# Low parts of weights and rotary products: from GpSimd to VectorE in a two-layer diffusion trunk

## The chip, the cores and the metric

The kernel runs on one core of a Trainium2 chip. The metric is the device time of one execution in microseconds; the number to predict is the median of several runs. Engines are named as in the profile: PE (TensorE), ACT (ScalarE), DVE (VectorE), POOL (GpSimd) and SP (SyncE, which issues the DMAs here).

## The reference

Two layers run over 256 latent tokens (`x`) and 256 context tokens (`h`), 1024 wide, in float32. Each layer is three sub-layers: a feed-forward layer, a mixing layer, a feed-forward layer.

```python
x = ffn_sublayer(x, mod_x, 0, *f0)
h = ffn_sublayer(h, mod_h, 0, *f0)

ax = adaln_in(x, norm_pre[l, 1], mod_x[:, 3], mod_x[:, 4])
ah = adaln_in(h, norm_pre[l, 1], mod_h[3], mod_h[4])
uv_x, qb_x, qc_x, kb_x, vb_x, kc_x, vc_x = jnp.split(ax @ w_in[l], SPLITS, axis=-1)
...
qb_x = apply_rope(qb_x.reshape(b_, l_, B_HEADS, 2, B_QK_DIM), cos_b, sin_b)
...
o_a = chunk_gmlp(uv_x, ...)            # gated spatial mixing
o_b = diff_post(diff_attention_latent(qb_x, k_all, v_all, lam), ...)
o_c = swa_latent(qc_x, kc_x, vc_x, kc_h, vc_h, sink)
mix_x = jnp.concatenate([o_a, o_b, o_c], axis=-1) @ w_out[l]
x = adaln_out(x, mix_x, norm_post[l, 1], mod_x[:, 5], 1.0)
...
x = ffn_sublayer(x, mod_x, 2, *f1)     # (silu(y @ wg) * (y @ wu)) @ wd, half residual weight
```

The rotary embedding is `x * cos + rot * sin`, on latent queries and keys alone. In the second layer the context gives keys and values only.

## The kernel before

**Three products for one.** Every weight tile of 2048 columns is loaded by SP into a staging buffer (`stg`, three of them) and then split: ACT writes the rounded high part `hi` (line 240), and a subtraction writes the low part `lo = full - hi` (`split_lo`, line 101). A matrix product is then three matmuls into one PSUM bank: `hi` by `Yh`, `lo` by `Yh`, `hi` by `Yl`, where `Yh` and `Yl` are the activations split in the same way. `acc3` issues the three terms at lines 250 and 254, `acc3_multi` at 263 (the second term), 269 and 271. `split` cuts a tile with eight or more blocks into four pieces and smaller ones into two; for each piece it issues the ACT copy and then the subtraction.

**Who subtracts.** The subtraction is on DVE, but where `share=True` is passed the first piece of the tile is on POOL: for the tiles of the input projection (`cols`, and the three tiles `wv` of the values), for those of the output projection of the first layer (`chunk` in `mixing`), and for the first two pairs of gate and up tiles of every feed-forward layer but the first (`two` in `ffn`, lines 614 and 618). A piece is 512 columns in most of them, 1024 for the output projection, 640 for `wv`, 256 for the narrow key tile.

**Rotary.** `rope_evac` (line 701) takes a 256 column product out of PSUM with ACT, shuffles it on DVE (704), multiplies the shuffled copy by the sine on DVE (705), multiplies the original by the cosine on POOL (706), and adds the two on DVE (707).

**What else POOL does.** The power -1/2 of each norm on one to four columns (lines 424, 839, 920, 1187), the product of one half of a feed-forward output with its gate row (line 521, `hf` 0), and the DMAs that store the gate rows (379).

**Softmax and residual on DVE.** A unit of differential attention reduces the scores on DVE (800), lets ACT take the exponent (802), combines two sums in two instructions on one or two columns (805, 806) and blends the two exponent tiles (808); PE then transposes the blend (781), ACT takes it out of PSUM (783), and PE multiplies it by the values (818). The windowed attention does the same with lines 872 to 880 and 895. `residual` adds the scaled product to the stream (439) and scales the normed stream (447), with a root from POOL ahead of each; `turn_y` transposes the result on PE (461) and splits it again (466, 471, 101).

**Order.** Each engine runs its own queue in order. The order within a queue is fixed when the program is built, from program order, from the `high_priority` blocks (which hold the splits of the input projection, `first=True`), and from the estimates of the planner that lays out the queues. On PE the attention units, rotary and transposes are interleaved with the projections by a clock written out in the kernel (`later`, `tick`, `task`).

Of the kernel before, what the change touches and what calls it, by code (L numbers as in the profile page):

```python
# [15 lines left out]
ALU = mybir.AluOpType  # L16
# [9 lines left out]
KB = D // P  # L26
# [37 lines left out]
def trunk(ctx: ExitStack, tc: tile.TileContext, x, c, cx, c_ctx, w_mod, b_mod, norm_pre, norm_post,  # L64
          w_gate, w_up, w_down, w_in, w_out, v_gain, w_s, b_s, diff_lambda, diff_subln, swa_sink,
          rope, out):
    nc = tc.nc
# [29 lines left out]
    def f32(ap):  # L97
        return ap.bitcast(F32)

    def split_lo(lo, full, hi, eng=nc.vector):  # L100
        eng.tensor_tensor(lo, full, f32(hi), op=ALU.subtract)  # L101


    evq, clk, busy = [], [0.0], [False]
# [114 lines left out]
                return split(v, *args[1:], **kw)  # L219
        return split(stage(*args), *args[1:], **kw)  # L220

    def split(v, nk, ncol, pair=False, into=None, share=False, pool=False):
        if into is not None:
            hi, lo = into
        else:
            hi = wsp.tile([P, 2048], F32R, tag="hi", name=nm("hi"))[:, 0:nk * ncol].rearrange(
                "p (k c) -> p k c", k=nk)
            lo = wsp.tile([P, 2048], F32R, tag="lo", name=nm("lo"))[:, 0:nk * ncol].rearrange(
                "p (k c) -> p k c", k=nk)
        if pair:  # L230
            v4 = v.rearrange("p k (v g d) -> p k v g d", v=2, g=2)
            for g in range(2):
                hv = hi[:, :, g * P:(g + 1) * P].rearrange("p k (v d) -> p k v d", v=2)
                lv = lo[:, :, g * P:(g + 1) * P].rearrange("p k (v d) -> p k v d", v=2)
                nc.scalar.activation(hv, v4[:, :, :, g, :], AF.Copy)
                split_lo(lv, v4[:, :, :, g, :], hv)
            return hi, lo
        cut = [0, nk // 4, nk // 2, nk // 2 + nk // 4, nk] if nk >= 8 else [0, nk // 2, nk]
        for a, b in zip(cut, cut[1:]):
            nc.scalar.activation(hi[:, a:b, :], v[:, a:b, :], AF.Copy)  # L240
            split_lo(lo[:, a:b, :], v[:, a:b, :], hi[:, a:b, :],
                     nc.gpsimd if pool or (share and a == 0) else nc.vector)
        return hi, lo

    def acc3(o, terms):
# [299 lines left out]
                task(("y", s), turn_y(ys, nxt, st, s[0], *((pb, T_LATE, 1.2) if s == order[-1] else (pa,))))  # L545


    def gate_up(l, e, cs, into=None, share=False):
        return (wchunk([(0, 256, w_gate[l, e, :, cs:cs + 256])], KB, 256, into=into, share=share),
                wchunk([(0, 256, w_up[l, e, :, cs:cs + 256])], KB, 256, share=share))  # L550

    def gate_up_one(l, e, cs):
        return wchunk([(0, P, w_gate[l, e, :, cs:cs + P]), (P, 256, w_up[l, e, :, cs:cs + P])], KB, 256)
# [1 line left out]
    def ffn(l, e, streams, nxt, first=None, out_order=None):  # L555
        j = 2 * e
        full = (streams[-1][0], streams[0][1])
        n = full[1] - full[0]
# [33 lines left out]
        for pi, (f0, nf) in enumerate(PHASES):  # L592
            Uh = big.tile([P, KB, NT], F32R, tag="Uh", name=nm("Uh"))
            Ul = big.tile([P, KB, NT], F32R, tag="Ul", name=nm("Ul"))
            for fp in range(0, nf, 2):
                cs = (f0 + fp) * P
                two = pi == 0 and fp == 0 and not first
                if pi == 0 and fp == 2 and not first:
                    continue
                rows = nxt is None  # L600
                if first and pi == 0 and fp == 0:
                    for i in range(3):
                        hidden(first[i], first[3 + i], i, full)
                    step()
                    continue
                if first and pi == 0 and fp == 2:
                    gu = [pa(), pa()]
                    w = gate_up_one(l, e, cs + P)
                    for i in range(2):
                        acc3(gu[i], yterms(w, i * P, full))  # L610
                    hidden(gu[0], gu[1], 3, full)
                    step()
                    continue
                wg, wu = gate_up(l, e, cs, share=two)
                if two:
                    into = [t[:, 4:8, :].rearrange("p a (b c) -> p (a b) c", b=2)
                            for t in (Uh, Ul)]
                    second = gate_up(l, e, cs + 256, into, True)
                    for s in range(2) if rows else streams:
                        drain(("y", s))  # L620
                        for f, (g_, u_) in ((0, (wg, wu)), (2, second)):
                            if rows:
                                gu = pa()
                                acc3_multi([(gu[:, c0:c0 + 256], rterms(w, s), c0 == 0)
                                            for w, c0 in ((g_, 0), (u_, 256))])
                                task("u", hidden_rows(gu, f, s))
                                continue
                            gus = [pa(), pa()]
                            groups = []
                            for w, c0 in ((g_, 0), (u_, 256)):  # L630
                                for i in range(2):
                                    groups.append((gus[i][:, c0:c0 + 256], yterms(w, i * P, s),
                                                   c0 == 0))
                            acc3_multi(groups)
                            for i in range(2):
                                hidden(gus[i][:, 0:256], gus[i][:, 256:512], f + i, s)
                else:
                    for i in range(2):
                        g = pa()
                        acc3(g[:, 0:n], yterms(wg, i * P, ys))  # L640
                        u = pa()
                        acc3(u[:, 0:n], yterms(wu, i * P, ys))
                        hidden(g[:, 0:n], u[:, 0:n], fp + i, full)
                step()

            drain("u")
            down(l, e, pi, f0, nf, Z, Uh, Ul, out_order or streams, nxt)
# [40 lines left out]
    def mixing(l, streams, qstreams, nxt):  # L688
# [4 lines left out]
        full = (0, NT)  # L693
# [4 lines left out]
        W = w_in[l]  # L698


        def rope_evac(dst, ps, scale):
            nc.scalar.activation(dst, ps, AF.Copy, scale=scale)
            sh = wk.tile([P, 256], F32, tag="t256", name=nm("shf"))
            nc.vector.stream_shuffle(sh, dst, shmask)
            nc.vector.tensor_tensor(sh, sh, ropet[:, 1, :], op=ALU.mult)
            nc.gpsimd.tensor_tensor(dst, dst, ropet[:, 0, :], op=ALU.mult)
            nc.vector.tensor_tensor(dst, dst, sh, op=ALU.add)

        def fm(w, f0, s):
# [10 lines left out]
                nc.scalar.activation(dst[:, SEQ:NT], ps[:, o:o + CTX], AF.Copy, scale=scale)  # L720

        def cols(c0, n, into=None):
            return wchunk([(0, n, W[:, c0:c0 + n])], KB, n, into=into, share=True, first=True)

        tmpw = big.tile([P, 2, KB, 256], F32R, tag="Ul", name=nm("tmpw"))
        wkq = []
# [21 lines left out]
        def rows_of(k0, n, c0, w):  # L748
            return W[k0 * P:(k0 + n) * P, c0:c0 + w]

        wv = [wchunk([(0, 512, rows_of(k0, n, VB0, 512)), (512, 640, rows_of(k0, n, VC0, P))], n, 640,
                     share=True, first=True)
              for k0, n in ((0, 3), (3, 3), (6, 2))]

        def tok_terms(ws, tb, c0, c1):
# [370 lines left out]
            return (QK[:, 4 + 2 * i:6 + 2 * i, SEQ:NT] if i < 2 else CU[:, 2 * i - 3:2 * i - 1, SEQ:NT])  # L1126

        def chunk(hf, i):
            return wchunk([(0, 512, w_out[l, i * 512:(i + 1) * 512, hf * 512:(hf + 1) * 512])], 4, 512,
                          share=True)  # L1130

        def oterms(ws, tb):
            return [(Yh[:, k, ycols(tb)], Yl[:, k, ycols(tb)], ws[k // 4][0][:, k % 4, :],
# [195 lines left out]
```

## Time and profile before

| | |
|---|---|
| median of 3 runs | 1762.75 us (1761.02 to 1763.5) |
| the profiled execution: its own time, its span | 1762.98 us, 1761.2 us |
| PE matmul busy | 1722.4 us, 98% |
| DVE, ACT, POOL busy | 1190.4, 696.3, 168.9 us |
| mixing layer of layer 0, attention and output (480 to 600 us) | PE busy 113.37 of 120 us |
| end of mixing of layer 1 and first tiles of its feed-forward layer (1550 to 1575 us) | PE busy 21.63 of 25 us |

How to read it: the span is that of the instructions; the time of a run has 1.78 us around it. PE works almost throughout, so what a change can give back is the time in which PE waits. Those waits lie at the edges of stages and in the mixing layers. A row of a timeline has the start, the time taken, the engine, the line, out<-in, the shape and the count of instructions merged; in brackets stands the idle time of the engine before it and what ended that.

### The profile page before, as it was taken

Reading aid. Unit: us, or ns where it says so; the run is one execution under the profiler, and the core shown is the slowest. Engines: PE = TensorE matmul, PEld = TensorE weight load, DVE = VectorE, ACT = ScalarE, POOL = GpSimd, SP = SyncE. Lnnn points to the kernel's source line nnn. Section 1 sums busy time; section 2 is a strip of 40 time slices with the busy share of each in tenths; the row PEclk is TensorE's granted clock in tenths of the full one; section 3 lists DMA queues with packets and bytes.
Section 4 is the critical chain, followed back from the end, with each engine's and each line's share of the span. In section 5 each row is a group of like instructions: output and inputs, shape, how many; then the busy total and the mean of one; then the engine's idle time right before and its main releaser. Section 6 shows DMA issues by size and latency. Waiting matters only on the chain.

```text
span 1761.2 us, 24837 instructions
## 1 busy us (share of the span) xinstructions
PE 1722.4 (98%) x9663; PEld 1449.9 (82%) x9663; DVE 1190.4 (68%) x2174; ACT 696.3 (40%) x1480; POOL 168.9 (10%) x185
## 2 busy tenths in 40 slices
PE   7999999999999999999999999999999999999998
PEld 5788888879977789888888898888888897689997
DVE  4876876775667576768766576777864756765555
ACT  4332322244376562333232442332223526655443
POOL 0000000021322120000000210000001321010000
PEclk9999999999999999999999999999999999999999
DMA  9654554543131143445545233655544133226552
GB/s 336 207 173 160 188 197 144 167 150 109 60 103 52 57 137 125 162 163 189 191 144 185 75 120 123 205 178 191 180 144 167 48 108 120 73 90 197 192 191 84
DMA packets 197105, 259.20 MB, mean 147 GB/s; under 512 B 8234, under 2 KB 132348, under 8 KB 196988
## 3 DMA queue, kind: packets, MB, share of 16 engines
q1 hardware_dynamic: 195452, 257.56, 44.3%
q8 instruction: 76, 1.25, 0.3%
q14 instruction: 41, 0.34, 0.1%
q0 software_dynamic: 1536, 0.05, 0.0%
HBM read 256.49 MB, written 1.10 MB: 146 GB/s over the span
## 4 chain that ended last, share of the span: by engine, by line
PE 63%; DVE 7%; ACT 2%; issue 2%; POOL 1%; DMA 1%; POOLq 0%; DVEq 0%; ACTq 0%
PE pa L250 19%; PE pa L254 9%; PE pb L269 4%; PE pb L271 4%; PE pb L263 4%; PE pa L263 4%; PE pa L271 4%; PE pa L269 4%; PE pb L250 3%; DVE lo L101 2%; PE pb L254 1%; PE pa L797 1%; PE pc L818 1%; PE pc L895 1%; DVE S L439 1%
## 5 line engine op out<-in xcount | busy, mean ns | idle before, releaser
L101 DVE TENSOR_TENSOR lo<-stg,hi 128x512 fp32r<-128x512 f32 (+3 forms) x476 | 367.0, 807 | 192.5 <-ACT hi L240 122.8
L240 ACT ACTIVATE hi<-stg 128x512 fp32r<-128x512 f32 (+3 forms) x496 | 318.4, 702 | 329.6 <-PE pa L263 97.2
L250 PE MATMUL pa<-Yh,hi 128*128 128x512 f32 (+1 forms) x1168 | 415.0, 365 | 0.0
L250 PE MATMUL pa<-Yl,hi 128*128 128x512 f32 (+1 forms) x1168 | 413.8, 364 | 0.0
L357 DVE SCALAR_TENSOR_TENSOR acc<-stg,sT,acc 128x512 f32<-128x512 f32 x448 | 305.2, 743 | 4.0 <-DMA stg<-in_w_mod_dram 4.0
L254 PE MATMUL pa<-Yh,lo 128*128 128x512 f32 (+1 forms) x1168 | 257.8, 363 | 0.0
L250 PEld LDWEIGHTS pa<-Yh,hi 128*128 128x128 f32 x1168 | 220.5, 189 | 36.6 <-issue 2.9
L250 PEld LDWEIGHTS pa<-Yl,hi 128*128 128x128 f32 x1168 | 220.5, 189 | 35.0 <-issue 1.2
L254 PEld LDWEIGHTS pa<-Yh,lo 128*128 128x128 f32 x1168 | 202.4, 189 | 34.3
L570 ACT ACTIVATE Uh<-ha 128x512 fp32r<-128x512 f32 (+1 forms) x92 | 50.7, 551 | 296.4 <-DVE ha L568 296.4
L263 PE MATMUL pb<-hi,Ul 128*128 128x512 f32 x400 | 156.9, 392 | 0.0
L271 PE MATMUL pb<-lo,Uh 128*128 128x512 f32 x400 | 155.9, 390 | 0.8 <-DVE lo L101 0.8
L269 PE MATMUL pb<-hi,Uh 128*128 128x512 f32 x400 | 155.8, 391 | 0.1
L568 DVE TENSOR_TENSOR ha<-ha,pa 128x512 f32<-128x512 f32 (+1 forms) x91 | 53.0, 583 | 79.5 <-PE pa L254 79.0
L269 PE MATMUL pa<-Yh,hi 128*128 128x256 f32 x368 | 92.0, 285 | 0.0
L271 PE MATMUL pa<-Yl,hi 128*128 128x256 f32 x368 | 91.3, 283 | 0.0
L271 PEld LDWEIGHTS pb<-lo,Uh 128*128 128x128 f32 x400 | 75.1, 188 | 16.6 <-DVE lo L101 1.3
L263 PEld LDWEIGHTS pb<-hi,Ul 128*128 128x128 f32 x400 | 75.1, 188 | 16.5 <-issue 1.2
L269 PEld LDWEIGHTS pb<-hi,Uh 128*128 128x128 f32 x400 | 75.2, 188 | 16.0 <-DVE Z L503 0.5
L566 ACT ACTIVATE ht<-pa 128x512 f32<-128x512 f32 (+1 forms) x91 | 46.3, 510 | 104.1 <-PE pa L254 81.8
L379 POOL DMA_DIRECT2D gate<-gr x48 | 24.3, 513 | 603.7 <-DVE gr L376 535.3
L567 DVE SCALAR_TENSOR_TENSOR ha<-ht,pa 128x512 f32<-128x512 f32 (+1 forms) x91 | 52.9, 581 | 37.2 <-ACT ht L566 36.4
(299 smaller groups left out, 2732.4 us busy)
## 6 DMA issues: line engine op xcount, KB each, us to landing
stg<-in_w_mod_dram SPq DMA_DIRECT2D x64, 1024.0 KB, 5.0
stg<-in_ffn_w_gate_dram SPq DMA_DIRECT2D x42, 1024.0 KB, 5.2
stg<-in_ffn_w_up_dram SPq DMA_DIRECT2D x42, 1024.0 KB, 5.1
stg<-in_ffn_w_down_dram SPq DMA_DIRECT2D x32, 1024.0 KB, 5.0
stg<-in_w_in_dram SPq DMA_DIRECT2D x14, 1024.0 KB, 4.8
stg<-in_ffn_w_down_dram SPq DMA_DIRECT2D x16, 768.0 KB, 4.4
mst<-in_w_mod_dram SPq DMA_DIRECT2D x16, 512.0 KB, 7.6
stg<-in_w_out_dram SPq DMA_DIRECT2D x8, 1024.0 KB, 6.4
```

The source lines that it names most:

```text
L101: eng.tensor_tensor(lo, full, f32(hi), op=ALU.subtract)
L240: nc.scalar.activation(hi[:, a:b, :], v[:, a:b, :], AF.Copy)
L250: nc.tensor.matmul(o, lhsT=ah, rhs=r, start=(i == 0), stop=(i == n - 1))
L254: nc.tensor.matmul(o, lhsT=al, rhs=bh, start=(i == 0), stop=(i == n - 1))
L263: nc.tensor.matmul(o, lhsT=al, rhs=bh, start=False, stop=last, skip_group_check=True)
L269: nc.tensor.matmul(o, lhsT=ah, rhs=bh, start=(first and k == 0), stop=False, skip_group_check=True)
L271: nc.tensor.matmul(o, lhsT=ah, rhs=bl, start=False, stop=False, skip_group_check=True)
L357: nc.vector.scalar_tensor_tensor(a, v[:, k, :], sc, a, op0=ALU.mult, op1=ALU.add)
L566: nc.scalar.activation(t, g, AF.Tanh, scale=0.5)
L567: nc.vector.scalar_tensor_tensor(a, t, 1.0, g, op0=ALU.add, op1=ALU.mult)
L568: nc.vector.tensor_tensor(a, a, u, op=ALU.mult)
L570: nc.scalar.activation(uh, a, AF.Copy)
```

## The change

`split_lo` loses its engine argument and always runs on DVE; `split` loses `share` and `pool`; `wchunk` callers lose `share=True`; and the cosine product of the rotary embedding goes to DVE. Nothing is removed from the computation, and shapes, tiles, DMAs and PE's instructions are as before. 37 subtractions and 22 rotary products move. POOL keeps the roots, the gate products of line 521, and its DMAs.

```diff
-    def split_lo(lo, full, hi, eng=nc.vector):
-        eng.tensor_tensor(lo, full, f32(hi), op=ALU.subtract)
+    def split_lo(lo, full, hi):
+        nc.vector.tensor_tensor(lo, full, f32(hi), op=ALU.subtract)
...
-    def split(v, nk, ncol, pair=False, into=None, share=False, pool=False):
+    def split(v, nk, ncol, pair=False, into=None):
...
-            split_lo(lo[:, a:b, :], v[:, a:b, :], hi[:, a:b, :],
-                     nc.gpsimd if pool or (share and a == 0) else nc.vector)
+            split_lo(lo[:, a:b, :], v[:, a:b, :], hi[:, a:b, :])
...
-                wg, wu = gate_up(l, e, cs, share=two)
+                wg, wu = gate_up(l, e, cs)
...
-                    second = gate_up(l, e, cs + 256, into, True)
+                    second = gate_up(l, e, cs + 256, into)
...
-            nc.gpsimd.tensor_tensor(dst, dst, ropet[:, 0, :], op=ALU.mult)
+            nc.vector.tensor_tensor(dst, dst, ropet[:, 0, :], op=ALU.mult)
...
-            return wchunk([(0, n, W[:, c0:c0 + n])], KB, n, into=into, share=True, first=True)
+            return wchunk([(0, n, W[:, c0:c0 + n])], KB, n, into=into, first=True)
...
-                     share=True, first=True)
+                     first=True)
...
-            return wchunk([(0, 512, w_out[l, i * 512:(i + 1) * 512, hf * 512:(hf + 1) * 512])], 4, 512,
-                          share=True)
+            return wchunk([(0, 512, w_out[l, i * 512:(i + 1) * 512, hf * 512:(hf + 1) * 512])], 4, 512)
```

## Rows read from the trace of the kernel before

**Rows 1.** The first part of the page: busy time of each engine, share of the span, instructions.

```profile
PE 1722.4 (98%) x9663; PEld 1449.9 (82%) x9663; DVE 1190.4 (68%) x2174; ACT 696.3 (40%) x1480; POOL 168.9 (10%) x185
```

**Rows 2.** POOL's instructions grouped by line and shape over the whole span: busy time and mean ns of one, then the idle time before them. All but the second row are instructions that move.

```profile
L101 POOL TENSOR_TENSOR lo<-stg,hi 128x512 fp32r<-128x512 f32 x19 | 28.3, 1489 | 35.4 <-ACT hi L240 35.4
L424 POOL TENSOR_TENSOR r<-v,negh 128x1 f32<-128x1 f32 x38 | 26.4, 694 | 114.8 <-DVE v L422 108.5 <-DMA stg<-in_w_in_dram 6.3
...
L101 POOL TENSOR_TENSOR lo<-stg,hi 128x640 fp32r<-128x640 f32 x6 | 13.6, 2271 | 28.1 <-ACT hi L240 28.1
L706 POOL TENSOR_TENSOR QK<-QK,ropet 128x256 f32<-128x256 f32 x16 | 13.3, 850 | 13.4 <-DVE shf L704 13.4
L101 POOL TENSOR_TENSOR lo<-stg,hi 128x1024 fp32r<-128x1024 f32 x5 | 12.2, 2446 | 32.9 <-ACT hi L240 32.9
...
L706 POOL TENSOR_TENSOR CU<-CU,ropet 128x256 f32<-128x256 f32 x6 | 5.7, 946 | 27.1 <-DVE shf L704 27.1
L101 POOL TENSOR_TENSOR Ul<-stg,Uh 128x512 fp32r<-128x512 f32 x3 | 4.3, 1426 | 2.0 <-DVE zg L1083 1.2 <-ACT Uh L240 0.8
L101 POOL TENSOR_TENSOR tmpw<-stg,tmpw 128x512 fp32r<-128x512 f32 x2 | 2.9, 1446 | 0.5 <-ACT tmpw L240 0.5
...
L101 POOL TENSOR_TENSOR lo<-stg,hi 128x256 fp32r<-128x256 f32 x2 | 1.5, 731 | 58.8 <-ACT hi L240 58.8
```

**Rows 3.** DVE's instructions in the same view: the subtractions by shape, the two rotary instructions that stand on either side of POOL's product, and a product of two 128x256 tiles elsewhere (line 921).

```profile
L101 DVE TENSOR_TENSOR lo<-stg,hi 128x512 fp32r<-128x512 f32 x369 | 242.7, 699 | 115.5 <-ACT hi L240 63.3 <-PE pa L254 51.4 <-PE pb L254 0.8
L101 DVE TENSOR_TENSOR lo<-stg,hi 128x1024 fp32r<-128x1024 f32 x87 | 106.7, 1240 | 31.4 <-PE pa L254 16.9 <-ACT hi L240 14.3 <-ACT hi L235 0.2
...
L705 DVE TENSOR_TENSOR shf<-shf,ropet 128x256 f32<-128x256 f32 x22 | 18.6, 871 | 0.1
...
L707 DVE TENSOR_TENSOR QK<-QK,shf 128x256 f32<-128x256 f32 x16 | 10.0, 652 | 0.1
...
L921 DVE TENSOR_TENSOR VG<-VG,r 128x256 f32<-128x256 f32 x6 | 2.5, 425 | 4.8 <-POOL r L920 4.8
...
L101 DVE TENSOR_TENSOR lo<-stg,hi 128x640 fp32r<-128x640 f32 x2 | 1.7, 826 | 1.9 <-ACT hi L240 1.6 <-issue 0.3
```

**Rows 4.** Three of PE's waits over the whole span: who waited for whom, us in total, times, longest.

```profile
PE pa L781 <- DVE p L808: 2.9, 4, 1.5
...
PE pa L271 <- DVE lo L101: 2.0, 2, 1.5
...
PE pb L461 <- DVE Z L447: 1.7, 2, 1.4
```

**Rows 5.** Busy time by stretch: PE, PEld, DVE, ACT, POOL, each with its count, then the granted clock of PE (1.00 is 2.4 GHz, 0.50 is 1.2 GHz), DMA share, GB/s. Attention and output of the mixing layer of layer 0; attention of layer 1; the end of mixing of layer 1 with the first feed-forward tiles behind it; and two pieces of 10 us of the last.

```profile
480.00:600.00 120.00, 113.37 (x753) 89.56 (x752) 84.86 (x232) 81.75 (x251) 22.17 (x17) 1.00 0.18 62
1456.00:1512.00 56.00, 51.64 (x337) 41.37 (x337) 41.52 (x92) 37.33 (x95) 10.93 (x9) 1.00 0.34 114
...
1550.00:1575.00 25.00, 21.63 (x148) 20.25 (x147) 18.02 (x26) 13.24 (x33) 7.22 (x6) 0.93 0.48 158
...
1560.00:1570.00 10.00, 7.13 (x53) 6.52 (x54) 8.36 (x15) 3.91 (x9) 2.64 (x3) 1.00 0.91 310
1570.00:1580.00 10.00, 10.00 (x73) 10.00 (x73) 4.33 (x10) 3.67 (x10) 0.00 (x0) 0.83 0.27 79
```

**Rows 6.** Timeline at 522 us, windowed attention in layer 0: a POOL subtraction, a DVE instruction on one column beside it, and PE's wait three steps on.

```profile
522.54 2.39 POOL L101 TENSOR_TENSOR lo<-stg,hi 128x1024 fp32r<-128x1024 f32 x1 [4.04 <-ACT hi L240]
...
522.67 2.27 DVE L875 TENSOR_TENSOR mx<-mx,nsink 128x1 f32<-128x1 f32 x1
...
526.11 1.10 PE L895 MATMUL pc<-VG,pT 128*128 128x64 f32 x8 [0.65 <-ACT pT L783]
```

**Rows 7.** Timeline at 560 and at 570 us, differential attention in layer 0: the one-column instruction of line 806, and PE's wait for line 808 behind it, twice.

```profile
560.83 1.60 DVE L806 SCALAR_TENSOR_TENSOR rs<-rs,nlam,ss 128x1 f32<-128x1 f32 x1
...
563.28 0.66 PE L781 MATMUL pa<-ident,p 128*128 128x128 f32 x4 [0.61 <-DVE p L808]
...
570.38 1.49 DVE L806 SCALAR_TENSOR_TENSOR rs<-rs,nlam,ss 128x1 f32<-128x1 f32 x1
...
572.72 0.66 PE L781 MATMUL pa<-ident,p 128*128 128x128 f32 x4 [1.50 <-DVE p L808]
```

**Rows 8.** Timeline at 1432 us, layer 1, the last tile of the values: POOL's subtraction and the matmul that waits for it.

```profile
1432.77 2.21 POOL L101 TENSOR_TENSOR lo<-stg,hi 128x640 fp32r<-128x640 f32 x1 [3.70 <-ACT hi L240]
...
1435.03 0.41 PE L250 MATMUL pb<-lo,Yh 128*128 128x320 f32 x1 [0.49 <-POOL lo L101]
```

**Rows 9.** Timeline of DVE from 1552 to 1566 us, with PE's longest wait behind it; the last row is a pair of line 439 at 1029 us, with no POOL instruction beside it, for comparison.

```profile
1552.29 2.39 DVE L101 TENSOR_TENSOR Yl<-yf,Yh 128x512 fp32r<-128x512 f32 x2
1554.61 2.40 DVE L101 TENSOR_TENSOR lo<-stg,hi 128x512 fp32r<-128x512 f32 x2
...
1557.54 3.58 DVE L101 TENSOR_TENSOR lo<-stg,hi 128x512 fp32r<-128x512 f32 x4
1561.03 1.88 DVE L101 TENSOR_TENSOR Ul<-stg,Uh 128x512 fp32r<-128x512 f32 x3
...
1563.72 2.43 DVE L439 SCALAR_TENSOR_TENSOR S<-zg,r,S 128x512 f32<-128x512 f32 x2
...
1569.37 0.39 PE L271 MATMUL pa<-lo,Yh 128*128 128x256 f32 x1 [1.50 <-DVE lo L101]
...
1028.85 1.42 DVE L439 SCALAR_TENSOR_TENSOR S<-Z,r,S 128x512 f32<-128x512 f32 x2 [0.45 <-POOL r L424]
```

More of the change, by code (lines that the diff above doesn't have):

```diff
@@ L545, in down, with gate_up @@
                 task(("y", s), turn_y(ys, nxt, st, s[0], *((pb, T_LATE, 1.2) if s == order[-1] else (pa,))))
-    def gate_up(l, e, cs, into=None, share=False):
-        return (wchunk([(0, 256, w_gate[l, e, :, cs:cs + 256])], KB, 256, into=into, share=share),
-                wchunk([(0, 256, w_up[l, e, :, cs:cs + 256])], KB, 256, share=share))
+    def gate_up(l, e, cs, into=None):
+        return (wchunk([(0, 256, w_gate[l, e, :, cs:cs + 256])], KB, 256, into=into),
+                wchunk([(0, 256, w_up[l, e, :, cs:cs + 256])], KB, 256))
     def gate_up_one(l, e, cs):
```

## The prediction

> **What bounds the kernel now.** I read the page first, then PE's waits, then the busy times by stretch, then the timelines of DVE and POOL around each wait. The page says that PE is busy 98% of the span [rows 1]. PE's instructions do not change, so all that the change can give is time in which PE waits: 1761.2 - 1722.4 = 38.8 us. The waits of PE that DVE ends are few and short: 2.9 us for the blended exponents, 2.0 us for low parts, 1.7 us for the scaled stream [rows 4]. By stretch, PE stands still 120 - 113.37 = 6.6 us in the attention of layer 0, 56 - 51.64 = 4.4 us in that of layer 1, and 25 - 21.63 = 3.4 us where layer 1 goes from mixing to feed-forward [rows 5]. So the whole matter is one of a few us in some 1760, and the question at each wait is what DVE was doing ahead of it.
>
> The timelines answer that. At 522.67 an instruction on one column takes DVE 2.27 us, while POOL works 2.39 us at a subtraction that began just before it; both end within 0.01 us [rows 6]. The same is seen at 560.83 and 570.38, where one-column instructions take 1.60 and 1.49 us [rows 7]. The rotary sine product takes 871 ns on DVE where an equal product of two SBUF tiles takes 425 ns, and the rotary sum 652 ns [rows 3]. So a POOL instruction does not run beside DVE's in these stages: DVE stands and waits for it. What the split of work between the two was to save is lost again in DVE, and with interest, since POOL is slower: 2446 ns against 1240 for a piece of 1024 columns, 2271 against 826 for 640, 1489 against 699 for 512, 850 to 946 against 425 for the rotary product [rows 2, 3].
>
> The Trainium skill says so in "SBUF — State Buffer", section "Who interferes with whom": a DVE instruction with two SBUF inputs and a POOL instruction that reads SBUF exclude each other, and the one that starts second waits for all of the first. The trace agrees, with the 2.27 us. The same rule speaks against the change as well, since it has no preferred side: what stays on POOL can be held up by what now comes to DVE. That is the second rival below.
>
> **The change part by part.**
>
> *Load.* DVE gets 24 pieces of 512 columns (19 + 3 + 2), 6 of 640, 5 of 1024, 2 of 256 and 22 rotary products: 24 x 0.70 + 6 x 0.83 + 5 x 1.24 + 2 x 0.425 + 22 x 0.425 = 16.8 + 5.0 + 6.2 + 0.9 + 9.4 = 38.2 us [rows 2, 3]. POOL loses 28.3 + 13.6 + 13.3 + 12.2 + 5.7 + 4.3 + 2.9 + 1.5 = 81.8 us [rows 2]. What DVE gets back is the time that it now stands behind those: in the rotary groups alone 22 x (0.871 - 0.425) + 16 x (0.652 - 0.425) = 9.8 + 3.6 = 13.4 us [rows 3], and 1.5 to 2.3 us at each place of rows 6 and 7. DVE's sum thus changes by something between +38 us (nothing comes back) and 38.2 - 81.8 = -44 us (DVE stood through all of POOL's time); I take about zero, since at the places of rows 6 and 7 a piece that costs DVE 1.24 us had held it for some 1.5 to 2.3. A busy sum is no time, though: what counts is below.
>
> *Attention of layer 0.* At 522 the one-column instruction waited 2.27 us for POOL. After the change the piece stands in DVE's own queue for at most 1.24 us, so the next step of ACT starts some 1.0 us earlier, and PE's wait of 0.65 us goes [rows 3, 6]: -0.65, between 0 and that. At 560 the wait of 1.60 becomes at most 1.24, less what the piece had already run: between 0.36 and 0.61 of PE's 0.61 us, and I take 0.6 [rows 7]. At 570 PE waits 1.50 us behind 1.49 us of DVE; with the piece ahead in the queue 0.6 us comes back (a piece that starts when POOL's did ends 1.2 us sooner, and the reciprocal and the two instructions behind it then run one after the other), with the piece behind it all 1.5: I take 0.6 [rows 7].
>
> *Values of layer 1.* At 1432 POOL needs 2.21 us for 640 columns and PE waits 0.49 us for it. DVE needs 0.83 us for each of the tile's two pieces, so both would be done at 1432.8 + 1.7 = 1434.5, when PE now begins to wait (1435.03 - 0.49): -0.5, between 0 and 0.5 [rows 3, 8].
>
> *End of mixing, layer 1.* Here DVE is what ends last from 1552 to 1569. Eight pieces in three groups took 2.39 + 2.40 + 3.58 = 8.37 us, where three pieces in a row with POOL at rest took 1.88, so 0.63 each: 8 x 0.63 = 5.0, which makes 3.4 us of standing. The pair of line 439 took 2.43 us against 1.42 undisturbed: 1.0 more [rows 9]. Four moved pieces come into that queue, 4 x 0.63 = 2.5. Net 3.4 + 1.0 - 2.5 = 1.9 us earlier. I take -1.6, because the last of the pieces may land ahead of the residual; the ends are 0 and the 3.4 us that PE stands there in all [rows 5, 9].
>
> *First feed-forward tiles elsewhere.* PE waits 1.7 us in all for line 447 [rows 4], at the end of mixing or feed-forward layers where one or two pieces move and one pair of line 439 or 447 is stretched. By the figures above a piece costs 0.6 and a stretch 1.0, so a few tenths come back at each: -0.5, between +0.5 and -1.7.
>
> *Rotary.* The four instructions now follow each other on one engine, 0.425 us each instead of 0.871 and a wait for POOL. PE has the values to multiply meanwhile, which hide them; if they did not, the rotary chain would still be the shorter one. 0. If the cover went, the gain would be up to 22 x 0.45.
>
> *Queues passed.* No DMA moves. POOL's queue gets emptier, so roots no longer stand behind a piece whose weights have not landed (6.3 us in one place [rows 2]). On DVE a first piece that waits for ACT's `hi` holds what is behind it, which is softmax work; but the second piece of the same tile stood there already and waited for a later `hi`. 0, with the bound in the third rival.
>
> *Sum.* 0.65 + 0.6 + 0.6 + 0.5 + 1.6 + 0.5 = 4.45 us. The profiled execution took 1762.98 us, 0.23 above the median, so 1762.98 - 4.45 - 0.23 = **1758.3 us** as a median.
>
> **The rivals.**
>
> *The clock stays up: faster still.* From 1570 to 1580 the granted clock is 0.83, so part of the stretch is at 1.2 GHz, right after 10 us in which PE was busy only 7.13 [rows 5]. That is 10 x 0.17 = 1.7 us lost. If the shorter waits ahead of it spare the fall, 1758.3 - 1.7 = 1756.6. For it: the waits ahead shrink by half. Against it: half remain.
>
> *Nothing to be had (no change).* The pieces run one after the other wherever they are, and ACT or a root is next. ACT is busy 81.75 of 120 us in the attention [rows 5], and the step right ahead of PE is ACT's at 526 [rows 6]. Roots take 694 ns in the mean [rows 2] and can be held by one DVE piece of 0.70 us, half of it on average; some six roots stand ahead of the waits for line 447 and of the end of mixing: 6 x 0.35 = 2.1. If that is paid, and the attention gives nothing but the 0.65 of 522 us, the sum is 4.45 - 1.2 - 2.1 = 1.2, hence 1761.6. For it: POOL's roots lie on the path of every residual. Against it: the DVE pieces are shorter than POOL's. The skill's page "Perfetto Trace Analysis", section "Optimizing Scalar/DVE Operations", leans this way: since the two engines share a port, moving work between them might not help. No run here shows the move yet.
>
> *The queue of DVE (slower).* While POOL holds it, DVE can still run what reads PSUM; while DVE works at a piece itself, nothing passes it. If the pieces come to lie ahead of the reductions of scores, each is paid by PE. In the two attention stretches nine move: 3 of 1024, 4 of 512, 2 of 256, which is 3 x 1.24 + 4 x 0.70 + 2 x 0.425 = 7.4 us [rows 3]. It decides once more than the 4.45 is paid so; all of it with no gain elsewhere gives 1770, with the gains outside the attention (2.6) 1767.5. For it: DVE is busy 41.52 of 56 us in the attention of layer 1 and has no idle ahead of several reductions. Against it: what held DVE there was POOL for longer than the piece takes. A planner that lays the queues in another order belongs here too.
>
> **How the numbers follow.** A measurement of this kernel can tell about 0.2% from no change, 3.5 us: faster is under 1759.2, slower over 1766.3. The forecast has 0.37 and the clock case 0.17, which makes 0.54 for faster; no change has 0.33, between 1759.2 and 1766; slower 0.13. The range: the upper bounds of all terms (0.65 + 0.61 + 1.5 + 0.5 + 3.4 + 1.7 + 1.7 of the clock = 10.1) give 1752.7, all at once is unlikely, so 1753.5; upwards it takes in the case of no change and stops short of the slow one, 1764.5.
>
> **What would show it.** Right: lines 806, 808 and 875 at 0.15 to 0.75 us throughout; line 705 near 0.42; POOL busy near 168.9 - 81.8 = 87 us; DVE's sum within some 10 us of before; the waits of rows 6 to 8 gone, PE busy above 22.5 of 25 at the end of mixing in layer 1. Wrong: reductions (800, 874) that start later with a subtraction right ahead of them, roots that take over 1 us, or DVE's sum up by 30 us. Then the standing was not POOL's doing, and the forecast falls.

## The result, and the profile after

The kernel after the change takes 1751.03 us (median of 6 runs, 1748.82 to 1752.95), the kernel before beside it 1762.32 us (6 runs, 1759.7 to 1763.5): ratio 0.9935, 95% interval 0.9924 to 0.9946, so 11.3 us less. The direction was forecast, the size was not: 4.45 us had been taken, and 1751.03 lies below the range. The profiled execution took 1751.76 us, with a span of 1750.0 us. Lines of the kernel after stand one lower than in the kernel before from about line 242 on, two lower from about 1130 on. The experiments keep the old numbers.

The first part of the page answers to [rows 1]:

```profile
PE 1722.0 (98%) x9663; PEld 1450.9 (83%) x9663; DVE 1180.3 (67%) x2233; ACT 696.3 (40%) x1480; POOL 92.6 (5%) x126
```

POOL lost 168.9 - 92.6 = 76.3 us, and DVE, which took over 59 instructions, became 10.1 us *shorter* in its sum. The groups by line and shape show where (busy us, mean ns of one, then the idle time ahead and what ended it). First POOL's, to [rows 2]: the roots, and the gate product that stays.

```profile
L423 POOL TENSOR_TENSOR r<-v,negh 128x1 f32<-128x1 f32 x38 | 26.7, 702 | 164.1 <-DVE v L421 164.1
L520 POOL TENSOR_TENSOR Z<-Z,gp 128x512 f32<-128x512 f32 x14 | 24.6, 1760 | 583.8 <-ACT pb L519 583.8
```

Then DVE's, to [rows 3]:

```profile
L101 DVE TENSOR_TENSOR lo<-stg,hi 128x512 fp32r<-128x512 f32 x388 | 251.1, 690 | 113.4 <-ACT hi L240 59.3 <-PE pa L253 51.5 <-PE pb L253 2.6
...
L704 DVE TENSOR_TENSOR shf<-shf,ropet 128x256 f32<-128x256 f32 x22 | 9.2, 416 | 0.0
...
L706 DVE TENSOR_TENSOR QK<-QK,shf 128x256 f32<-128x256 f32 x16 | 6.7, 416 | 0.1
```

The rotary sine product is at 416 ns (871 before), the rotary sum too (652 before). Roots are where they were, 702 ns against 694. PE's waits, to [rows 4]: that for line 447 of before is gone, the low parts are down from 2.0 to 0.8 and 0.4, and the blend of exponents stays at 2.8, with a longest of 1.8 where it was 1.5.

```profile
PE pa L780 <- DVE p L807: 2.8, 4, 1.8
...
PE pb L270 <- DVE lo L101: 0.8, 1, 0.8
...
PE pa L270 <- DVE lo L101: 0.4, 1, 0.4
```

Busy time by stretch, to [rows 5] (same columns; the stretches are moved by what was gained ahead of them):

```profile
480.00:600.00 120.00, 115.25 (x770) 91.22 (x770) 83.48 (x244) 83.33 (x256) 8.20 (x8) 1.00 0.20 65
1450.00:1506.00 56.00, 53.34 (x331) 43.32 (x330) 41.04 (x97) 37.07 (x95) 4.15 (x3) 0.94 0.34 114
1543.00:1568.00 25.00, 24.53 (x187) 23.35 (x186) 19.11 (x38) 15.86 (x40) 1.42 (x2) 1.00 0.48 158
1553.00:1563.00 10.00, 9.53 (x78) 9.09 (x77) 8.82 (x18) 4.14 (x11) 1.42 (x2) 1.00 0.91 301
1563.00:1573.00 10.00, 10.00 (x85) 9.97 (x84) 4.76 (x11) 5.57 (x16) 0.00 (x0) 1.00 0.22 79
```

The end of mixing of layer 1 has lost 2.9 of its 3.4 us of standing, and the clock behind it is 1.00 where it was 0.83. In the attention of layer 1 the clock is lower than before, 0.94.

**A ledger by place.** PE runs nearly the same list of matmuls in all these kernels, so the start of the n-th matmul can be compared with that in the profile before; how the difference grows within a stretch is what the stretch gained (-) or lost (+). Stretches are in us of the profile before; those left out changed by 0.5 or less in every column. One profiled execution each.

```
             after   e12    e1    e2    e3    e4    e5    e9    e6   e11   e10
   0-485      0.30 -0.55 -1.23 -0.35 -1.74 -1.20 -1.63 -0.10 -1.91  0.57 -1.92
 485-655     -2.75 -2.31 -0.17  0.03 -1.95 -0.28 -0.14 -0.22 -0.17 -1.85 -4.61
 655-662     -0.83 -0.83 -0.83  0.00 -0.77  0.01  1.88 -0.23  0.00 -0.83 -0.83
1026-1038    -2.57 -2.15 -2.16 -0.84 -0.85 -0.82  0.89 -0.73 -0.03 -2.15 -2.57
1400-1475    -1.66 -1.63  0.02 -1.69  0.02  1.35 -0.06 -0.01  0.01 -1.63 -1.68
1490-1508     1.50  1.58  0.00  0.12  1.77  1.43  1.74  1.77 -0.01 -0.14 -0.27
1558-1571    -3.75 -3.76 -3.76  0.54  0.19  0.02 -0.07 -2.18 -1.74 -1.68 -3.74
1571-1580    -1.20 -1.19 -1.19 -0.53 -0.23 -0.01 -1.20 -1.19 -1.24 -1.22 -1.19
```

Three rows must be read with care. The first 485 us differ by up to 2.5 us between executions, and by 0.85 between two of the same program (after and e12), so that row is not the change's. Most of it arises in the first 25 us, where no instruction differs: before, e2 and e9 have a granted clock of 0.61 to 0.65 from 20 to 24 us and the others 1.00; in after, e11 and e12 the 28 matmuls of line 302 (301 after) at 16 us take 2.89 to 3.08 us, in all the others 1.92. In the row 485 to 655, e3, e11 and e12 have a fall of the clock (0.57 to 0.69 from 570 to 574 us). The row 1490 to 1508 is the clock, below. The column "after" without its first row comes to -11.3 (-11.1 with the stretches left out), as the medians have it.

### The profile page after: what moved, and what is told of

It reads as the page before. It is cut to its first block, busy times and chain, and to the rows that moved or that the text cites. A ratio compares the mean times of both kernels' runs of the same rounds, so it can differ in the third digit from the quotient of the medians.

```text
span 1750.0 us, 24754 instructions
## 1 busy us (share of the span) xinstructions
PE 1722.0 (98%) x9663; PEld 1450.9 (83%) x9663; DVE 1180.3 (67%) x2233; ACT 696.3 (40%) x1480; POOL 92.6 (5%) x126
## 4 chain that ended last, share of the span: by engine, by line
PE 90%; DVE 5%; ACT 2%; DMA 1%; issue 1%; POOL 1%; SPq 0%; POOLq 0%; DVEq 0%; ACTq 0%
PE pa L249 26%; PE pa L253 13%; PE pb L262 6%; PE pb L268 6%; PE pa L262 6%; PE pb L270 6%; PE pa L270 6%; PE pa L268 6%; PE pb L249 3%; PE pb L253 2%; PE pa L1252 1%; PE pa L796 1%; DVE acc L356 1%; PE pc L894 1%; DVE lo L101 1%; PE pc L366 1%
## 5 line engine op out<-in xcount | busy, mean ns | idle before, releaser
L101 DVE TENSOR_TENSOR lo<-stg,hi 128x512 fp32r<-128x512 f32 (+4 forms) x508 | 383.3, 794 | 194.7 <-ACT hi L240 106.0
L249 PEld LDWEIGHTS pa<-Yl,hi 128*128 128x128 f32 x1168 | 220.5, 189 | 35.1 <-issue 1.2
L270 PEld LDWEIGHTS pa<-Yl,hi 128*128 128x128 f32 x368 | 70.6, 192 | 0.1
```

Source lines behind the costliest of these rows:

```text
L101: nc.vector.tensor_tensor(lo, full, f32(hi), op=ALU.subtract)
L249: nc.tensor.matmul(o, lhsT=ah, rhs=r, start=(i == 0), stop=(i == n - 1))
L270: nc.tensor.matmul(o, lhsT=ah, rhs=bl, start=False, stop=False, skip_group_check=True)
```

## The experiments

**Which part brings it.** e1, e2, e3 and e4 each do one part of the change and leave the rest as before.

e1, the first feed-forward tiles:

```diff
-                wg, wu = gate_up(l, e, cs, share=two)
+                wg, wu = gate_up(l, e, cs, share=False)
...
-                    second = gate_up(l, e, cs + 256, into, True)
+                    second = gate_up(l, e, cs + 256, into, False)
```

> Only the first feed-forward tiles (the line that passes share=two and the one below it) lose their share on POOL; input tiles, output tiles and the rotary product stay as before. Theory A (each site pays its own wait for a POOL subtraction, and the prices add): the traces of before and after, laid beside each other by the n-th matmul, show these tiles at the turn at 658 us (1.1), at the turn at 1033 us (2.6), and at the end of mixing of layer 1 with the clock behind it (4.0 and 1.0), so 8.7 us less than before, 1752 to 1755. Theory B (my forecast's sizes): 0.5 and 1.6, so 2.1 us less, about 1760. Theory C (the gain comes from the planner laying out the queues in another order, which the whole change decides): no value between 0 and 11 is favoured, and the matmuls at those three places don't gain what they gained in after.

Measured: 1753.33 against 1762.51 us, ratio 0.9949 (0.9936 to 0.9962), 9.2 us less. In the ledger it has the three places of the expectation's theory A and the clock behind the last, as the whole change has them.

e2, the input tiles (`share=False` in `cols` and `wv`):

> Only the input projection's tiles (the column tiles and the three value tiles of each layer) lose their share on POOL. Theory A: the turn to mixing of layer 1 at 1408 us (0.5), the values of layer 1 at 1435 us (0.7), 1464 to 1472 us (0.5), so 1.7 us less, about 1760.6; attention of layer 0 not much changed. Theory B: 0.5 us less, about 1762. Theory C: a change at places that these tiles don't touch, such as the end of mixing of layer 1.

Measured: 1760.26 us, 0.9987 (0.9978 to 0.9996), 2.3 us less; 1.69 of it between 1400 and 1475 us, as A has it.

e3, the output tiles (`share=False` in `chunk`):

> Only the output projection's tiles lose their share on POOL. Theory A: what attention of layer 0 gained at 545 to 567 us, 1 to 2 us less than before, 1760.5 to 1761.5, and nothing at 1033 us. Theory B: 1.2 us less. Theory C: a change at places that these tiles don't touch.

Measured: 1758.3 us, 0.9977 (0.9968 to 0.9986), 4.2 us less: 1.95 in the attention of layer 0, and 0.8 at each of the two turns (from one sub-layer to the next, at 655 and 1026 us), where A had nothing for it.

e4, the rotary product alone (line 706 on `nc.vector`):

> Only the rotary product moves to VectorE; all subtractions stay as they were. Theories A and B: 0, at most 0.7 us less (500 to 545 us in attention of layer 0). Theory C: the product's place in the planner's costs moves the order of others, and the time goes either way by 1 to 2 us at places without a rotary product.

Measured: 1762.05 us, 0.9997 (0.9988 to 1.0006): no difference in the median. Moving it shortens DVE's own work (the 871 ns) and PE doesn't see that. By place it is not nothing, though: the ledger has 0.82 less at 1026 us and 1.35 more at 1408 us, ahead of the first rotary products. There a subtraction that stood behind two rotary products in POOL's queue now starts just ahead of the pair of line 447, which takes 2.14 us (0.88 before), and PE waits 1.58 us for that pair instead of 0.27:

```profile
1405.63 1.53 POOL L101 TENSOR_TENSOR lo<-stg,hi 128x640 fp32r<-128x640 f32 x1
1405.70 2.14 DVE L447 TENSOR_SCALAR Z<-S,r 128x512 f32<-128x512 f32 x2 [0.45 <-POOL r L424]
```

So where the rotary product leaves, the next subtraction comes into DVE's way at this place; the median hides it. It is one profiled execution.

The four medians add to 9.2 + 2.3 + 4.2 + 0.5 = 16.2, more than the whole. The ledger says what is counted more than once: 0.8 at 655 us in e1 and in e3, and 0.8 at 1026 us in e2, e3 and e4, none of which touches a tile there. The timeline at that turn shows how. Before, the profile has POOL's subtraction start between the two instructions of line 439, and the second then waits for it:

```profile
1020.41 2.46 DVE L439 SCALAR_TENSOR_TENSOR S<-Z,r,S 128x512 f32<-128x512 f32 x2 [0.44 <-POOL r L424]
...
1020.91 1.40 POOL L101 TENSOR_TENSOR lo<-stg,hi 128x512 fp32r<-128x512 f32 x1 [0.54 <-ACT hi L240]
...
1023.66 0.16 DVE L422 SCALAR_TENSOR_TENSOR v<-ss 128x1 f32<-128x1 f32 x1 [0.79 <-ACT Z L444]
```

In e4 the tile's `hi` comes 0.25 us later against DVE (0.75 us behind the start of the pair instead of 0.50), and it is POOL that waits, 1.83 us for its piece, while the pair takes 1.42:

```profile
1018.95 1.42 DVE L439 SCALAR_TENSOR_TENSOR S<-Z,r,S 128x512 f32<-128x512 f32 x2 [0.44 <-POOL r L424]
...
1019.70 1.83 POOL L101 TENSOR_TENSOR lo<-stg,hi 128x512 fp32r<-128x512 f32 x1 [0.78 <-ACT hi L240]
```

So who holds whom there hangs on a quarter of a microsecond, and one part of what the whole change removes can also go away by itself.

e7 puts e1 and e3 together.

> The feed-forward tiles and the output tiles lose their share on POOL; input tiles and rotary products stay. If the gains add: 9.2 + 4.2 = 13.4 us less, 1749.1. If what the two runs gained at 658 and 1033 us is the same time seen twice: 2 us less than that, 1751. If the whole change loses through the input tiles or the rotary products what the other two bring: below 1751, too.

Measured: 1752.87 against 1761.63 us, 0.995 (0.9937 to 0.9962), 8.8 us less. The parts don't add; the second case (1751) is nearest. Its interval doesn't separate it from the whole change.

**Holding by itself.** e5 has the tiles on DVE as e1 has, the same order on PE, ACT, DVE and SP, and lets POOL do the moved subtraction once more into a tile that nobody reads (18.1 us; the moved pieces were 168.9 - 151.9 = 17.0 us of POOL's). Nobody waits for a result of POOL's; its presence is back, and the staging buffers are freed as late as it makes them.

```diff
-                     nc.gpsimd if pool or (share and a == 0) else nc.vector)
+                     nc.gpsimd if pool or (share == 1 and a == 0) else nc.vector)
+            [split_lo(scr[:, 0:ncol], v[:, k, :], hi[:, k, :], nc.gpsimd) for k in range(a, b) if share == 2 and a == 0]
...
+                wg, wu = gate_up(l, e, cs, share=2 * two)
...
+                    second = gate_up(l, e, cs + 256, into, 2)
```

> As the run with only the feed-forward tiles moved, and besides POOL repeats each moved subtraction (two instructions of 256 columns in place of one of 512) into a scratch tile that nobody reads. The order of the queues of PE, ACT, DVE and SP is that of the run with only the feed-forward tiles moved; POOL's work is added and nobody waits for its result. Theory A1 (POOL holds DVE; that alone was the loss): the time goes back to that of before or beyond it, about 1762. Theory A2 (holding is a part, the other part is that the planner lays DVE's queue in another order): the pair of line 439 takes 2.4 us again at the turn at 1033 us, and the pieces at the end of mixing take longer than 0.63 us each, 2 to 5 us come back, 1755.5 to 1758.5. Theory C (order alone, or the lateness of POOL's results alone): 1753.3 stays.

Measured: 1765.53 against 1761.63 us, 1.0021 (1.0012 to 1.003): 3.9 us slower than before, 13 us over e1. The ledger has it at e1's three places (1.88 + 0.83 = 2.7, 0.89 + 2.16 = 3.1 and 3.76 - 0.07 = 3.7), and 1.7 at the clock. At the end of mixing, DVE and POOL of e5:

```profile
1557.98 2.46 POOL L101 TENSOR_TENSOR scr<-stg,hi 128x256 fp32r<-128x256 f32 x2 [0.49 <-POOL scr L101]
1559.17 5.30 DVE L101 TENSOR_TENSOR lo<-stg,hi 128x512 fp32r<-128x512 f32 x6
1560.52 2.20 POOL L101 TENSOR_TENSOR scr<-stg,Uh 128x256 fp32r<-128x256 f32 x2
```

and the same six pieces in the kernel after, with POOL at rest, followed by the root's input and the residual:

```profile
1549.52 3.69 DVE L101 TENSOR_TENSOR lo<-stg,hi 128x512 fp32r<-128x512 f32 x6
1553.13 0.68 DVE L101 TENSOR_TENSOR Ul<-stg,Uh 128x512 fp32r<-128x512 f32 x1
1553.73 0.15 DVE L421 SCALAR_TENSOR_TENSOR v<-ss 128x1 f32<-128x1 f32 x1
...
1554.61 1.42 DVE L438 SCALAR_TENSOR_TENSOR S<-zg,r,S 128x512 f32<-128x512 f32 x2
1555.94 1.89 DVE L101 TENSOR_TENSOR Ul<-stg,Uh 128x512 fp32r<-128x512 f32 x3
```

e9 halves the dose: one instruction of 256 columns in place of two.

```diff
+            [split_lo(scr, v[:, a:b, 0:P], hi[:, a:b, 0:P], nc.gpsimd) for k in range(1) if share == 2 and a == 0]
```

> As the run with the repeats (the feed-forward tiles on DVE, POOL repeats each moved subtraction into a tile that nobody reads), but each repeat is one instruction on half of the columns. The order of the queues of PE, ACT, DVE and SP is again that of the run with only the feed-forward tiles moved. If the loss is the time that POOL holds DVE: a single instruction of 256 columns should hold about a third to a half of what the pair of 256 did (2.2 us a pair in that run), so 3 to 6 of its 12 us come back, 1756 to 1760. If the loss in that run came from the number of starts (two per piece, with a handover each): about half again, so the same sum and no distinction. If the loss came from something else, such as the later release of the staging buffers: the sum stays near 1765.

Measured: 1758.13 against 1762.95 us, 0.9971 (0.996 to 0.9982), 4.8 less than before, so 4.4 us over e1 where e5 was 13. POOL's extra work is 8.9 us against 18.1. The loss goes with the dose, more than in proportion. That a late result of POOL's was the whole loss is excluded: nobody waits for one here. That it was a part is not: at the end of mixing PE waits for a low part of POOL's, 0.64 us before and 1.33 in e6. Nor is it excluded that the number of starts costs, and not the time held, or that later buffers have a part. At the end of mixing the timeline shows the holding itself: DVE's queue is the same, without idle, and its six pieces take 1.6 us more.

**Order by itself.** In the profile before, three pieces `Ul` of 1.88 us stand ahead of the root's input at 1561 us [rows 9]; after, they stand behind the residual, as shown above. POOL's holding and this order changed together. e6 is the kernel before with this order alone: POOL's and PE's queues are as before, DVE's differs at this place only, and so do three of ACT's copies there.

```diff
-                    second = gate_up(l, e, cs + 256, into, True)
+                    with (tc.issue_after(behind[0].ins) if nxt is None else nullcontext()): second = gate_up(l, e, cs + 256, into, True)
```

> The kernel before, all of POOL's work as it was; only at the end of mixing of layer 1 are the four pieces of the second gate tile put behind the last residual on DVE's queue (three of them are on DVE), as the whole change and the run with only the feed-forward tiles have them. Theory A1 (holding alone): nothing, 1762.5. Theory A2: the three pieces took 1.88 us ahead of the root's input, so the root comes 1.9 us sooner, 1.9 us less and up to 1.0 more if the clock doesn't fall behind it: 1759.6 to 1760.6. Theory C (order alone): the whole 5.3 us of that place, 1757.2.

Measured: 1759.96 against 1761.63 us, 0.9986 (0.9977 to 0.9995), 1.7 to 2.5 us less by medians or by ratio. The ledger has 1.74 at the place and 1.24 at the clock behind it: 3.0 of the 5.0 us there. Its timeline still has POOL's holding, the four pieces in 3.58 us and a one-column instruction in 1.26, and PE waits for POOL's piece:

```profile
1555.45 3.58 DVE L101 TENSOR_TENSOR lo<-stg,hi 128x512 fp32r<-128x512 f32 x4
1558.95 0.14 DVE L422 SCALAR_TENSOR_TENSOR v<-ss 128x1 f32<-128x1 f32 x1
...
1561.15 1.89 DVE L101 TENSOR_TENSOR Ul<-stg,Uh 128x512 fp32r<-128x512 f32 x3
1561.93 2.27 POOL L101 TENSOR_TENSOR lo<-stg,hi 128x512 fp32r<-128x512 f32 x1 [2.15 <-ACT hi L240]
1562.96 1.26 DVE L422 SCALAR_TENSOR_TENSOR v<-ss 128x1 f32<-128x1 f32 x1
...
1564.25 0.39 PE L271 MATMUL pa<-lo,Yh 128*128 128x256 f32 x1 [1.33 <-POOL lo L101]
```

So what e6 leaves of the place, 3.75 - 1.74 = 2.0 us, is by subtraction, and it holds both POOL's holding and the late piece. The whole change and e1 also have 20 of PE's matmuls there (1569 to 1573 us before) in another order, which e6 has not.

e11 was meant as the counterpart: the whole change with `second` laid out as urgent.

```diff
+                    with (tc.high_priority() if nxt is None else nullcontext()): second = gate_up(l, e, cs + 256, into, True)
```

> The whole change, with the second gate tile of the last feed-forward layer laid out as urgent, so that its four pieces stand ahead of the last residual on DVE's queue, as three of them did in the kernel before; POOL doesn't hold DVE there. The planner also lays some matmuls at that place in another order. If the queue's order has a price of its own without POOL: three pieces of 0.63 us ahead of the root's input, 1.9 us more, and up to 1.2 more if the clock falls: 1753 to 1754. If the order only mattered because POOL held DVE: 1751.

Measured: 1753.42 against 1762.95 us, 0.9944 (0.9931 to 0.9956), 9.5 us less. At 1558 us it gives 2.1 of 3.75 back, but not as expected. The planner put the four `Ul` ahead of other pieces, not ahead of the root's input, and PE waits for those others, 0.92 and 1.60 us. It shows that the order is worth 2 us there without POOL, and not that the order of before is.

**What is left.** e8 moves the gate product of line 521 to DVE as well.

> The whole change, and the gate product of line 521 that stays on POOL there goes to DVE as well, so POOL keeps the roots alone. If what is left of POOL's holding still costs time at the turns: up to 1 us less at each of four turns, 1747 to 1750. If those products stand beside DVE's work that nobody waits for: 1751. If they come into DVE's queue ahead of the sum of line 519: up to 0.7 us more at a turn, 1752 to 1754.

Measured: 1751.33 against 1761.63 us, 0.9937 (0.9925 to 0.995): the same as the whole change. POOL's 68.2 us are roots and DMAs, and nothing more comes back.

e10 takes up the one term that gave nothing. In the kernel after, a piece stands inside the blend at 570 us:

```profile
568.63 0.17 DVE L804 RECIPROCAL rs<-ss 128x2 f32<-128x2 f32 x1 [1.25 <-ACT p L801]
568.71 1.22 DVE L101 TENSOR_TENSOR lo<-stg,hi 128x1024 fp32r<-128x1024 f32 x1
569.85 0.21 DVE L805 SCALAR_TENSOR_TENSOR rs<-rs,nlam,ss 128x1 f32<-128x1 f32 x1
...
570.98 0.44 PE L780 MATMUL pa<-ident,p 128*128 128x128 f32 x2 [1.82 <-DVE p L807]
```

The edit ties one tile's pieces behind the blend (`blend[0]` is the instruction of line 808; old line numbers here):

```diff
+            with (tc.issue_after(blend[0].ins) if (hf, i) == (0, 0) else nullcontext()):
+                return wchunk([(0, 512, w_out[l, i * 512:(i + 1) * 512, hf * 512:(hf + 1) * 512])], 4, 512)
```

> The whole change, with the first half of one tile of the output projection (layer 0) put behind the blend of exponents on DVE's queue; in the profile after, a piece of 1.22 us stands between the reciprocal and the two instructions of the blend (568.71 to 569.85 us), and PE waits 1.8 us for that blend. If that queue order is why the term for 570 us gave nothing: the wait there falls by 1.0 to 1.4 us, 1749.8 to 1750.2 in the median, clear in the row and at the limit in the median. If the exponent is what ends last there: the wait stays 1.8. If the tile itself comes too late behind it: a new wait of PE for the low part, up to 2.4 us, and the time rises by up to 1.

Measured: 1745.91 (1745.71 to 1746.87) against 1762.95 us, 0.9904 (0.989 to 0.9917): 17 us under before, and 5.1 under after. The wait went from 1.82 to 1.20 us, 0.6 less where 1.0 to 1.4 was expected:

```profile
566.40 0.17 DVE L805 RECIPROCAL rs<-ss 128x2 f32<-128x2 f32 x1 [1.25 <-ACT p L802]
566.60 0.22 DVE L806 SCALAR_TENSOR_TENSOR rs<-rs,nlam,ss 128x1 f32<-128x1 f32 x1
...
567.66 0.66 PE L781 MATMUL pa<-ident,p 128*128 128x128 f32 x4 [1.20 <-DVE p L808]
```

The median was expected at 1749.8 to 1750.2. By the ledger the attention of layer 0 gained 1.9 more than after, of which 0.65 is there by 575 us and the rest by 590, where DVE's queue differs too; and the clock in layer 1 did not fall (1.8). The profiled executions differ by 2.2 more in the first 485 us, 1.8 of it in the first 25, where no instruction differs (the matmuls of line 302 above). So 1.9 us is placed at the stage that the edit touches; the rest is the clock and the start, and that the edit causes them is not shown.

e12 is the whole change once more.

> The whole change once more, for a second profile of the same program. If the fall of the clock in the attention of layer 1 (1490 to 1500 us in the profile after, 1.5 us there) and the first 100 us (0.6 us more than before there) belong to the execution and not to the program: another picture at those two places, and the same offsets as in the profile after within 0.1 us at 520 to 655, 655 to 662, 1028 to 1038, 1430 to 1437 and 1558 to 1580 us. If they belong to the program: the same at all places. Median 1751 either way, so the version with the piece behind the blend stays 4 to 5 us under it.

Measured: 1750.95 against 1761.67 us, 0.9939 (0.9925 to 0.9952). The start differs, and the clock in layer 1 falls here too, so that seems to belong to the program. The other places agree within 0.5 where 0.1 was expected. The two that are off by 0.4 have a reason: at 572 us the clock falls here and not in after; and ahead of the turn at 1026 us the other engine is held. In after, POOL's gate product of line 520 takes 5.74 us at 1007.86 and DVE's two pieces beside it 1.29; here the product (line 521) takes 1.80 us at 1007.43 and the two pieces 2.38.

## Why the prediction was right in direction and short in size

*Load* held: DVE's sum 10 us down where about zero was taken, POOL at 92.6 where 87 was expected. Most of the difference is the one gate product of 5.74 us, held by DVE; in e12, where it takes 1.80, POOL's sum is 88.8.

*Attention of layer 0* held in sum, and by luck: 0.65 + 0.6 + 0.6 = 1.85 taken, 2.3 to 2.75 measured between 485 and 655. Two of its three terms came, 0.80 at 526 us and 0.62 at 563; that for 570 us failed. In its place came 0.92 at 567 us that the sum didn't have: a wait of before that is put down to ACT, and is gone after.

```profile
567.26 1.16 PE L818 MATMUL pc<-VG,pT 128*128 128x128 f32 x8 [0.76 <-ACT pT L783]
```

The term for 570 had the piece "ahead in the queue" and 0.6 back; the piece lies inside the chain, and the wait grew from 1.50 to 1.82 (in e10, with the piece out of it, it is 1.20).

*Values of layer 1*: 0.5 taken; e2 has 1.7 from 1400 to 1475, of which the tile of [rows 8] is 0.75 and the turn into the layer another 0.5 that the sum didn't have; 0.4 more comes at 1472 us.

*End of mixing, layer 1* is the first step that failed: 1.6 taken, at most 3.4, and 3.75 came. The working for POOL's holding is not contradicted: it made 1.9, and 2.0 is what e6 leaves, by subtraction. Missing was a second term as large: 1.74 us for the planner's new order of DVE's queue. The prediction spoke of that order only as a harm, in the slower rival.

*The clock stays up*, the second case, came as well: 1.2 us where 1.7 was worked out. Its condition, the shorter waits ahead, does not decide it. In e6 they are shorter and the clock stays at 1.00; but in e5 PE's waits at this place are 3.7 us in all (3.4 before), the longest 2.43 (1.50 before), and the clock is at 1.00 behind them as well:

```profile
1570.81 0.38 PE L271 MATMUL pa<-lo,Yh 128*128 128x256 f32 x1 [2.43 <-DVE lo L101]
```

So the reason given for this case is not borne out, and why the clock stays up is open.

*First feed-forward tiles elsewhere* is the second step that failed: 0.5 taken, at most 1.7, and 0.83 at 655 us with 2.15 to 2.57 at 1026 us came, some 3.2 us; e5 shows that POOL's presence alone brings it back and more. The bound of 1.7 counted only the waits that the profile puts down to line 447. Two more at these turns are put down to ACT, and they shrank too, already in e1, where ACT's work is the same; with POOL's presence, in e5, the first of them is 2.49 us. The ledger has 0.78, 1.58 and 0.5 to 0.9 at the three:

```profile
658.98 0.66 PE L461 MATMUL pb<-ident,Z 128*128 128x128 f32 x4 [0.62 <-ACT yf L466]
...
1033.13 0.99 PE L461 MATMUL pb<-ident,Z 128*128 128x128 f32 x7 [1.41 <-DVE Z L447]
...
1036.27 0.66 PE L461 MATMUL pb<-ident,Z 128*128 128x128 f32 x4 [0.72 <-ACT yf L466]
```

The sizes were off as well. The term set 0.6 for a moved piece against 1.0 for a stretch. The stretch was there (2.46 to 1.41 us for the pair of line 439, before and after), but the piece cost less than 0.6: before, DVE waited 0.79 us for ACT's squares ahead of the next root's input (shown with e4); after, two pieces stand there and the input follows without idle.

```profile
1015.11 1.41 DVE L438 SCALAR_TENSOR_TENSOR S<-Z,r,S 128x512 f32<-128x512 f32 x2 [0.44 <-POOL r L423]
1016.44 1.28 DVE L101 TENSOR_TENSOR lo<-stg,hi 128x512 fp32r<-128x512 f32 x2
1017.65 0.15 DVE L421 SCALAR_TENSOR_TENSOR v<-ss 128x1 f32<-128x1 f32 x1
```

From the pair's start to that input it is 1023.66 - 1020.41 = 3.25 us before and 1017.65 - 1015.11 = 2.54 after.

*Rotary* 0: right in the median, by e4, as a sum of gains and losses at places that the term did not look at. *Nothing to be had* and *the queue of DVE* fall: roots stayed at 702 ns, and a moved piece ahead of what PE waits for was found at one place (570 us). The Trainium skill, in "Perfetto Trace Analysis", section "Optimizing Scalar/DVE Operations", has it that moving work between the two engines might not help, where the question is how to relieve a full DVE; here the move goes the other way and helped by 11.3 us, and the measurement decides. What the Trainium skill says in "SBUF — State Buffer", section "Who interferes with whom", of one engine waiting for all of the other's instruction, the trace agrees with, now both ways: 1.26 us of DVE behind POOL in e6, and one gate product of 5.74 us on POOL behind DVE at 1007.86 us after.

Three terms went over their own upper bounds (values 1.7 for 0.5, end of mixing 3.75 for 3.4, first tiles some 3.2 for 1.7), so that the time lies below even the 1752.7 of all bounds together. Unforeseen was the loss of 1.5 us at 1490 us. With it the places close: 2.75 + 0.83 + 2.57 + 1.66 + 3.75 + 1.20 - 1.50 = 11.3.

## What to carry to other kernels

When a slow engine's share goes back to the fast one, price three things at each place where the fast one ends last: the time that it stood, the pieces that fit into its gaps for nothing, and the order that the planner will now lay down, which at one place here was worth about as much as the standing. Count all the waits of the bottleneck at such a place, and not only those that the profile puts down to the fast engine: a wait that it puts down to a third engine can go as well. Then lay the two queues side by side before summing, and look for a piece inside a short dependent chain; the kernel with one such piece moved ran 5 us under the change itself, of which 1.9 could be placed at that stage.

## What the runs showed of the hardware that was not expected

The granted clock fell in the attention of layer 1 in some kernels (after, e3, e4, e5, e7, e8, e9, e12) and not in the others, after nearly the same wait of PE for ACT's line 783 (782 after). Before, a wait of 1.37 us, then:

```profile
1496.00:1500.00 4.00, 2.49 (x18) 2.02 (x18) 2.54 (x10) 3.19 (x7) 2.18 (x2) 1.00 0.00 0
1500.00:1504.00 4.00, 4.00 (x37) 4.00 (x36) 3.10 (x6) 1.31 (x3) 1.91 (x1) 1.00 0.13 21
```

After, a wait of 1.49 us, then 0.63 and 0.52, so 1.2 GHz for most of the next 8 us:

```profile
1488.00:1492.00 4.00, 2.37 (x17) 1.81 (x16) 2.44 (x11) 3.53 (x7) 2.23 (x2) 1.00 0.00 2
1492.00:1496.00 4.00, 4.00 (x24) 4.00 (x24) 3.10 (x6) 1.32 (x3) 1.91 (x1) 0.63 0.08 11
1496.00:1500.00 4.00, 4.00 (x22) 4.00 (x21) 2.72 (x8) 1.07 (x4) 0.00 (x0) 0.52 0.76 255
```

The length of the wait isn't what decides: e4 has 1.37 us and a clock of 0.50 from 1500 to 1504, e11 has 1.49 us and loses nothing there. What does stays open, here as behind the end of mixing, where e5 kept the clock after a wait of 2.43 us and the kernel before lost it after one of 1.50. A fall cost 1.4 to 1.8 us in six of the eight, 0.2 in e7 and nothing in e8; part is won back, since PE's next waits are shorter.

Which of the two engines is held can differ between two executions of one program (after and e12, at 1007 us). When it was POOL, its product, 1.29 us where nothing of DVE's is beside it, took 5.74 and ended 1.16 us behind a row of nine DVE instructions without idle (1007.21 to 1012.44 us): as far as POOL's spans tell, it was held through the whole row and not through one.
